# A feed-forward block in fp32: sums on VectorE, one buffer pool for both products, second factors form by form, and the finish written inside the last product

## The chip, the cores and the metric

The kernel runs on one core of a Trainium2 chip. The metric is the device time of one execution in microseconds (us). The core has TensorE (PE, matrix products into PSUM), VectorE (DVE), ScalarE (ACT), GpSimd (POOL), and SyncE (SP), whose queue issues the transfers between DRAM and SBUF here. The order of the instructions on each engine is fixed when the kernel is built, by the scheduler of the framework from the program's text, its priorities and its buffers; each engine takes its own instructions in that order and waits on semaphores for the others. PE runs at one of two clocks, 1.2 or 2.4 GHz; the profile shows the granted clock as a share of the higher one.

## The reference, cut to what matters

One encoder layer on x (1024 rows by 1024). The change touches the last of its three parts:

```python
h = _rms_norm(x, ffn_pre_norm)
gate, up = jnp.split(h @ w_ffn_in, 2, axis=-1)      # 1024 x 1024 by 1024 x 5632
y = (jax.nn.silu(gate) * up) @ w_ffn_out            # 1024 x 2816 by 2816 x 1024
x = x + _rms_norm(y, ffn_post_norm)
```

## The kernel before, in words

Each fp32 factor is split into two fp32r tiles, hi (a cast on ACT) and lo = raw - hi (a subtraction on DVE), and a product is hi*hi + lo*hi + hi*lo: three matmuls of 128x128 by 128x512. Both products use seven sub-products for eight (a Winograd form), so sums of blocks are needed in front of them and behind them.

First product, `ffn_in`: 22 groups (11 gate and up pairs), each a class `InGroup` with seven sub-products p1 to p7 of 12 matmuls. The weight's forms (A11, A12, A22, S1 to S4) are made for every group by `form` (hi L1382, lo L1383), their sums by POOL (L1402, 1403, 1409, 1413). The activation's forms (T1 to T4, B22) are made once by `FormSink.piece`, for each k of 4 in column pieces, with t1 and t3 on POOL and t2 and t4 on DVE. p1 and p2 of the first three groups need none of these and are done first (`first_forms`, `early = 3`). p1 is copied out by ACT (L1423) before p2 adds to the same PSUM bank. u1 (L1433), u2 (L1442) and the sums in `use` are DVE's. `send` writes seven activation forms of each pair to DRAM; its sums are POOL's (L1487 to L1497).

Second product, `ffn_out`: seven products n = 0 to 6 (A11*B11, A12*B21, S2*T2, S3*T3, S1*T1, A22*T4, S4*B22), each 11 steps over 4 row blocks j, 12 matmuls a step, 924 in all. `operands` loads an activation form (L1584), splits it (L1586 ACT, L1587 DVE), loads weight blocks, sums them on POOL for T1 to T4 (L1568 to L1579), and splits them (L1590 ACT, L1591 DVE). `use` adds a finished product from PSUM (L1619). In the last product `finish_tile` follows each j for rows 4+j and j: sum of squares (ACT), load of the residual (L1607), rstd (ten DVE instructions of 128x1, L73 to L80), a multiply by rstd and post norm on DVE (L1611), an add of the residual (L1612, POOL for one half of the columns, DVE for the other), and the store.

Ahead of `ffn_in` stands the last tile of `out_proj`: its norm and 16 transposes (L1068) give the last columns of the activation (hraw, evacuated by ACT, L1070). `ffn_in` and `ffn_out` have a pool of buffers each for activations and for weights.

Of the kernel before, what the change touches and what calls it, by code (L numbers as in the profile page):

```python
# [19 lines left out]
P = 128  # L20
# [1028 lines left out]
class FormSink:  # L1049
# [32 lines left out]
    def open(self, pl, n, k):  # L1082

        K = self.K
        for name in ("T1", "T2", "T3", "B22", "T4"):
            pair = []
            for p in "hl":
                if n:
                    pair.append(pl.tile([P, 512], F32R, name=f"x{name}{p}{k}"))
                    n -= 1  # L1090
                else:
                    pair.append(K.ap.tile([P, 512], F32R, tag="act", name="act_f", bufs=K.abufs))
            self.f.setdefault(name, []).append(tuple(pair))

    def piece(self, pl, k, s):

        K, nc = self.K, self.K.nc
        n = s.stop - s.start

        def put(name, k, src):  # L1100
            hi, lo = self.f[name][k]
            nc.scalar.copy(hi[:, s], src)
            nc.vector.tensor_sub(lo[:, s], src, hi[:, s].bitcast(F32))
        tmp = lambda name: pl.tile([P, n], F32, tag="as", name=name, bufs=3)
        b11, b12, b21, b22 = (self.raw[a][b][:, s] for a, b in ((k, 0), (k, 1), (k + 4, 0), (k + 4, 1)))
        t1, t2 = tmp("t1"), tmp("t2")
        nc.gpsimd.tensor_sub(t1, b12, b11)
        nc.vector.tensor_sub(t2, b22, t1)
        put("T2", k, t2)
        put("T1", k, t1)  # L1110
        t3 = tmp("t3")
        nc.gpsimd.tensor_sub(t3, b22, b12)
        put("T3", k, t3)
        t4 = tmp("t4")
        nc.vector.tensor_sub(t4, b21, t2)
        put("T4", k, t4)
        put("B22", k, b22)
# [229 lines left out]

def mmk(K, out, a, b, start):
# [10 lines left out]
class InGroup:  # L1359
# [6 lines left out]
    def __init__(self, K, fp, wp, hf, c0, use):  # L1366
        self.K, self.fp, self.wp, self.hf, self.c0, self.use = K, fp, wp, hf, c0, use
        self.w = {}

    def load(self):  # L1370
        K = self.K
        self.raw = []
        for kh in range(2):
            raw = self.wp.tile([P, 4, 256], F32, tag="wr", name="w_raw", bufs=3)
# [393 lines left out]
```

## Time and profile before

| | us |
|---|---|
| median of three runs (lowest, highest) | 2588.98 (2586.65, 2590.16) |
| the profiled execution, its own time | 2588.08 |
| its span | 2586.4 |
| first matmul of `ffn_in`, last one | 1874.72, 2325.03 |
| first matmul of `ffn_out`, last one | 2336.70, 2571.40 |

In the span 2467.4 us have PE busy. The part that the change touches is the last 712 us. All times below are microseconds from the span's start. A matmul's record lasts 0.39 us at full clock, but the next one starts 0.2269 us later; so PE's rate is read from starts. In the same way a row's duration on DVE or ACT overlaps the next row's by some 0.08 us, and the pitch from start to start is what a chain of them costs.

### The profile page before, as it was taken

Reading aid. Unit: us, or ns where it says so; the run is one execution under the profiler, and the core shown is the slowest. Engines: PE = TensorE matmul, PEld = TensorE weight load, DVE = VectorE, ACT = ScalarE, POOL = GpSimd, SP = SyncE. Lnnn points to the kernel's source line nnn. Section 1 sums busy time; section 2 is a strip of 40 time slices with the busy share of each in tenths; the row PEclk is TensorE's granted clock in tenths of the full one; section 3 lists DMA queues with packets and bytes.
Section 4 is the critical chain, followed back from the end, with each engine's and each line's share of the span. In section 5 each row is a group of like instructions: output and inputs, shape, how many; then the busy total and the mean of one; then the engine's idle time right before and its main releaser. Section 6 shows DMA issues by size and latency. Waiting matters only on the chain. (4 is left out here: it accounts for less than half of the span.)

```text
span 2586.4 us, 38885 instructions
## 1 busy us (share of the span) xinstructions
PE 2467.4 (95%) x13445; PEld 2011.7 (78%) x13445; DVE 1767.6 (68%) x4037; ACT 1068.3 (41%) x2807; POOL 747.0 (29%) x937
## 2 busy tenths in 40 slices
PE   7999999999999999999999999999979999998897
PEld 5787788788788777788877887887758888876776
DVE  7778787897887855765577567535596556645677
ACT  5236244544554534654463233223553333224343
POOL 3352111112111111422133014313154444422542
PEclk9999999999999999999999999999979999998999
DMA  6214323322322422412113323214333233318865
GB/s 200 86 46 122 77 52 76 101 57 67 97 61 62 97 69 86 135 54 73 62 61 112 105 87 129 97 49 139 111 118 114 94 106 106 102 61 285 278 217 173
DMA packets 294926, 273.12 MB, mean 106 GB/s; under 512 B 93344, under 2 KB 213961, under 8 KB 294729
## 3 DMA queue, kind: packets, MB, share of 16 engines
q1 hardware_dynamic: 294729, 270.64, 33.6%
q8 instruction: 106, 1.74, 0.3%
q14 instruction: 91, 0.75, 0.1%
HBM read 206.80 MB, written 63.77 MB: 105 GB/s over the span
## 5 line engine op out<-in xcount | busy, mean ns | idle before, releaser
L134 PE MATMUL mm<-act_hi,w_lo 128*128 128x512 f32 (+1 forms) x1216 | 481.1, 398 | 0.0
L133 PE MATMUL mm<-act_lo,w_hi 128*128 128x512 f32 (+1 forms) x1216 | 478.2, 395 | 0.0
L131 PE MATMUL mm<-act_hi,w_hi 128*128 128x512 f32 (+1 forms) x1216 | 332.1, 399 | 4.2 <-ACT act_hi L162 2.2
L115 POOL TENSOR_SCALAR w_hi<-w_raw 128x512 fp32r<-128x512 f32 x232 | 160.8, 708 | 410.8 <-PE mm L133 208.4
L134 PEld LDWEIGHTS mm<-act_hi,w_lo 128*128 128x128 f32 x1216 | 229.7, 189 | 37.4
L133 PEld LDWEIGHTS mm<-act_lo,w_hi 128*128 128x128 f32 x1216 | 229.5, 189 | 37.3
L131 PEld LDWEIGHTS mm<-act_hi,w_hi 128*128 128x128 f32 x1216 | 220.6, 190 | 45.2 <-ACT act_hi L162 3.1
L116 DVE TENSOR_TENSOR w_lo<-w_raw,w_hi 128x512 fp32r<-128x512 f32 x232 | 183.0, 808 | 59.7 <-POOL w_hi L115 52.8
L133 PE MATMUL mm<-w_lo,act_hi 128*128 128x512 f32 (+1 forms) x480 | 180.8, 382 | 0.0
L134 PE MATMUL mm<-w_hi,act_lo 128*128 128x512 f32 (+1 forms) x480 | 180.1, 381 | 0.0
L861 POOL TENSOR_SCALAR Pm<-Pm,sm 128x1024 f32<-128x1024 f32 (+1 forms) x96 | 89.1, 930 | 251.4 <-DVE sm L860 86.5
L459 DVE SCALAR_TENSOR_TENSOR acc<-xp,ccol,acc 128x1024 f32<-128x1024 f32 x96 | 124.0, 1292 | 4.6 <-ACT acc L456 3.7
L131 PE MATMUL mm<-w_hi,act_hi 128*128 128x512 f32 (+1 forms) x480 | 120.7, 387 | 3.7 <-POOL w_hi L115 2.6
L159 ACT CAST th<-tr 128x512 fp32r<-128x512 f32 x128 | 74.8, 588 | 105.5 <-PE tr L904 103.5
L1382 ACT CAST w_hi<-s 128x512 fp32r<-128x512 f32 x88 | 54.7, 622 | 146.4 <-PE g L1355 104.8
L133 PEld LDWEIGHTS mm<-w_lo,act_hi 128*128 128x128 f32 x480 | 91.6, 191 | 17.3
L134 PEld LDWEIGHTS mm<-w_hi,act_lo 128*128 128x128 f32 x480 | 91.5, 191 | 17.2
L131 PEld LDWEIGHTS mm<-w_hi,act_hi 128*128 128x128 f32 x480 | 86.1, 191 | 22.4 <-POOL w_hi L115 3.8
L160 DVE TENSOR_TENSOR tl<-tr,th 128x512 fp32r<-128x512 f32 x128 | 87.2, 684 | 17.5 <-ACT th L159 15.6
L1383 DVE TENSOR_TENSOR w_lo<-w_raw,w_hi 128x512 fp32r<-128x512 f32 x66 | 75.4, 1143 | 28.1 <-ACT w_hi L1382 28.0
L857 ACT ACTIVATE Pm<-sc,nm 128x512 f32<-128x512 f32 x128 | 87.1, 688 | 16.6 <-DVE nm L852 16.2
L850 DVE TENSOR_REDUCE mx<-sc 128x1 f32<-128x512 f32 x128 | 85.0, 681 | 4.3 <-PE sc L134 4.1
(474 smaller groups left out, 6120.2 us busy)
## 6 DMA issues: line engine op xcount, KB each, us to landing
w_raw<-in_w_ffn_out SPq DMA_DIRECT2D x121, 256.0 KB, 4.2
w_raw<-in_w_in SPq DMA_DIRECT2D x120, 256.0 KB, 3.2
w_raw<-in_w_ffn_in SPq DMA_DIRECT2D x50, 512.0 KB, 3.6
Gr<-grow SPq DMA_DIRECT2D x48, 256.0 KB, 3.5
a_raw<-afS SPq DMA_DIRECT2D x44, 256.0 KB, 3.4
afA<-sg SPq DMA_DIRECT2D x33, 256.0 KB, 2.0
afS<-as SPq DMA_DIRECT2D x33, 256.0 KB, 2.0
a_raw<-afA SPq DMA_DIRECT2D x33, 256.0 KB, 4.2
```

What stands on the lines that cost most here:

```text
L115: nc.gpsimd.tensor_scalar(hi[part], raw, 1.0, 1.0, op0=ALU.mult, op1=ALU.mult)
L116: nc.vector.tensor_sub(lo[part], raw, hi[part].bitcast(F32))
L131: nc.tensor.matmul(out, a[0], b[0], start=(i == 0), stop=False)
L133: nc.tensor.matmul(out, a[0], b[1], start=False, stop=False)
L134: nc.tensor.matmul(out, a[1], b[0], start=False, stop=(i == n - 1))
L159: nc.scalar.copy(hi, ps)
L160: nc.vector.tensor_sub(lo, ps, hi.bitcast(F32))
L459: nc.vector.scalar_tensor_tensor(acc, xp[:, j:j + T], tap(j), acc, op0=ALU.mult, op1=ALU.add)
L850: nc.vector.reduce_max(mx[:, j:j + 1], ps, axis=AX.X)
L857: nc.scalar.activation(Pm[:, j * w:(j + 1) * w], ps, AF.Exp, bias=nm, scale=scale, accum_out=sm[:, j:j + 1])
L861: nc.gpsimd.tensor_scalar(Pm, Pm, sm[:, 0:1], 1.0, op0=ALU.mult, op1=ALU.mult)
L1383: nc.vector.tensor_sub(lo, src, hi.bitcast(F32))
```

## The change

Five edits. All sums of the block go to VectorE, so POOL has nothing to do in it. One pool, "ffn", gives the buffers for both products (a ring of 48 tiles of 128x512, and three weight tiles for `ffn_in`). `FormSink` makes the second factors form by form: T2 of all four k, then T1, T3, T4 and B22, once for the first 256 columns and once for the last 256; before, it went k by k, and k = 2, 3 at full width. In `ffn_out` T1 is kept from the step that makes T2, so that product 4 loads 22 weight blocks fewer (99 for 121), and the post norm is loaded behind product 3. The finish is split: `square` (sum of squares, load of the residual, a multiply by post norm) and `finish_tile` (rstd and one instruction that multiplies by it and adds the residual); rows 4 to 7 and the first halves of rows 0 to 3 are written into the last product's loop.

```diff
+    def first_piece(self, s):
+        nc = self.K.nc
+        self.t = [ffn_tile(self.K, "t12") for k in range(4)]
+        for k in range(4):
+            b11, b12, b21, b22 = self.blocks(k, s)
+            t1, t2 = self.t[k][:, 0:256], self.t[k][:, 256:512]
+            nc.vector.tensor_sub(t1, b12, b11)
+            nc.vector.tensor_sub(t2, b22, t1)
+            self.put("T2", k, s, t2)
...
-        nc.gpsimd.tensor_add(s1, self.block(1, 0), self.block(1, 1))
-        nc.gpsimd.tensor_sub(s2, s1, self.block(0, 0))
+        nc.vector.tensor_add(s1, self.block(1, 0), self.block(1, 1))
+        nc.vector.tensor_sub(s2, s1, self.block(0, 0))
...
     groups[0].p1()
     groups[0].p2()
-    for k in range(2):
-        hf.open(fp, 10 - 8 * k, k)
-        hf.piece(fp, k, first)
+    hf.open()
+    hf.first_piece(first)
+    hf.other_pieces(first)
     finish()
     for G in groups[1:early]:
         G.p1()
         G.p2()
-    for k in range(2):
-        hf.piece(fp, k, last)
-    for k in range(2, 4):
-        hf.open(fp, 0, k)
-        hf.piece(fp, k, both)
+    hf.first_piece(last)
+    groups[0].forms()
+    hf.other_pieces(last)
...
+        if name == "T2":
+            t1[g], t2[g] = half_tile(K, "t1"), ffn_tile(K, "t2")
+            nc.vector.tensor_sub(t1[g], weight(g, 0, 1), weight(g, 0, 0))
+            nc.vector.tensor_sub(t2[g], weight(g, 1, 1), t1[g])
+            return t2[g]
...
+    def square(t, ch):
+        part = acc[t // 4, ch, t % 4]
...
+        row_ssq(K, part, ssq[t][:, ch:ch + 1], xt[t, ch])
+        nc.sync.dma_start(xt[t, ch], K.x2[t * P:(t + 1) * P, ch * 512:(ch + 1) * 512])
+        nc.vector.tensor_mul(part, part, post[ch])
+
     def finish_tile(t):
...
+        rs = rstd1(K, ssq[t])
         for ch in range(2):
...
+            o = xt[t, ch]
+            nc.vector.scalar_tensor_tensor(o, acc[t // 4, ch, t % 4], rs, o, op0=ALU.mult, op1=ALU.add)
...
             for j in range(4):
                 ps = banks[n % 2][j](K)
                 for g, (a, b) in enumerate(ab):
                     step(ps, j, a, b, g)
+                if j == 0:
+                    second_half(4)
+                    for t in range(4):
+                        square(t, 0)
                 use(n, j, ps)
-                finish_tile(4 + j)
+                square(j, 1)
                 finish_tile(j)
+                if j < 3:
+                    second_half(5 + j)
...
-        with pool(K, "ffi") as fp, pool(K, "ffiw", "right") as wp:
-            ffn_in(K, sink, finish, fp, wp)
-        with pool(K, "ffo") as fp, pool(K, "ffow", "right") as wp:
-            ffn_out(K, fp, wp, out)
+        with pool(K, "ffn") as K.fp:
+            ffn_in(K, sink, finish)
+            ffn_out(K, out)
```

In the rows that follow, lines of the kernel after have their own numbers: L1404 is the cast of a weight form, L1095 and L1096 the cast and the lo of an activation form, L1441 the copy of p1, L1485 the silu of the first gate block, L1609 to L1611 the matmuls of `ffn_out`, L1621 the multiply by post norm, L1627 the multiply and add of the finish, L1634 the add of a finished product.

ScalarE where `ffn_in` begins, before (hraw are the evacuated last columns, p the copies of p1, t and hraw what activation forms are cast from):

```order
L1070 ACTIVATE hraw<-tr,cols 128x256 x5
L1382 CAST w_hi<-w_raw 128x512
L1423 COPY p_19939<-mm 128x512
L1102 CAST xT2h_19957<-t_19966 128x256
L1102 CAST xT1h_19955<-t_19965 128x256
L1382 CAST w_hi<-w_raw 128x512
...
L1467 ACTIVATE sg<-mm 128x512
L1102 CAST act_f<-t_19994 128x256
L1423 COPY p_20052<-mm 128x512
L1102 CAST act_f<-t_20001 128x256
L1423 COPY p_20080<-mm 128x512
```

The same place after:

```order
L1070 ACTIVATE hraw<-tr,cols 128x256 x8
L1404 CAST w_hi<-w_raw 128x512 x6
L1441 COPY p_19936<-mm 128x512
L1485 ACT_TABLE_LOAD
L1485 ACTIVATE sg<-mm 128x512
L1095 CAST part<-t_19992 128x256
L1095 CAST act_f<-t_19993 128x256
...
L1095 CAST part<-t_19995 128x256
L1095 CAST part<-hraw 128x256 x6
L1441 COPY p_20093<-mm 128x512
L1441 COPY p_20121<-mm 128x512
```

The casts of activation forms moved from in front of the first silu to behind it, and the copies of p1 for the second and third group moved behind all 24 casts of the first 256 columns.

TensorE in the last product, before (mm_25350 is the bank of j = 0, mm_25435 of j = 1; the two steps at the end of j = 0 and the start of j = 1):

```order
L1596 MATMUL mm_25350<-w_hi_25346,act_hi_25340 128x512
L1597 MATMUL mm_25350<-w_lo_25347,act_hi_25340 128x512
L1598 MATMUL mm_25350<-w_hi_25346,act_lo_25341 128x512
L1596 MATMUL mm_25435<-w_hi_25226,act_hi_25220 128x512
L1597 MATMUL mm_25435<-w_lo_25227,act_hi_25220 128x512
L1598 MATMUL mm_25435<-w_hi_25226,act_lo_25221 128x512
```

The same product after (mm_25274, mm_25399, g_25479 and tr_25559 are the banks of j = 0 to 3):

```order
L1609 MATMUL mm_25274<-w_hi_25150,act_hi_25146 128x512
L1609 MATMUL mm_25399<-w_hi_25150,act_hi_25146 128x512
L1609 MATMUL g_25479<-w_hi_25150,act_hi_25146 128x512
L1609 MATMUL tr_25559<-w_hi_25150,act_hi_25146 128x512
L1610 MATMUL mm_25274<-w_lo_25151,act_hi_25146 128x512
L1611 MATMUL mm_25274<-w_hi_25150,act_lo_25147 128x512
```

Before, a row block took its 33 matmuls one after the other; now every step goes over all four, and the four sums end within the last eight matmuls.

VectorE at the end of the last product, after (u and c are parts of rows 4 to 7 and of the first halves, one the sums that the last product completes, h and r the small tiles of rstd):

```order
L1621 TENSOR_TENSOR c_23902<-c_23902,post 128x512
L77 TENSOR_SCALAR h_25317<-h_25317 128x1
L1621 TENSOR_TENSOR c_23904<-c_23904,post 128x512
L79 SCALAR_TENSOR_TENSOR h_25317<-r_25318,h_25317 128x1
L1634 TENSOR_TENSOR one<-mm,one 128x512
L80 SCALAR_TENSOR_TENSOR r_25318<-h_25317,r_25318 128x1
L73 TENSOR_SCALAR h_25358<-ssq_25333 128x1
L1634 TENSOR_TENSOR one<-mm,one 128x512
```

The first add of the last product stands behind six multiplies and five small instructions of the finish; the other 10 multiplies, 75 small instructions and all 16 multiply-and-adds stand behind it.

## Rows read from the trace of the kernel before

**Rows 1.** The page: busy time and share of each engine, and the span in 40 slices for PE and its granted clock.

```profile
PE 2467.4 (95%) x13445; PEld 2011.7 (78%) x13445; DVE 1767.6 (68%) x4037; ACT 1068.3 (41%) x2807; POOL 747.0 (29%) x937
PE   7999999999999999999999999999979999998897
PEclk9999999999999999999999999999979999998999
```

**Rows 2.** Windows of the last part: the stretch and its length, then busy us and instructions of each engine, the granted clock, the DMA engines' share and GB/s.

```profile
1895.00:1900.00 5.00, 5.00 (x23) 3.94 (x21) 4.37 (x9) 2.57 (x9) 2.73 (x4) 1.00 0.33 105
1900.00:1935.00 35.00, 21.14 (x61) 13.59 (x61) 35.00 (x42) 15.85 (x30) 22.28 (x15) 0.71 0.24 76
1950.00:2000.00 50.00, 50.00 (x222) 41.44 (x221) 31.80 (x38) 15.56 (x26) 25.99 (x19) 1.00 0.34 116
2340.00:2345.00 5.00, 5.00 (x17) 3.92 (x17) 3.77 (x7) 3.58 (x6) 0.00 (x0) 0.68 0.98 364
2410.00:2415.00 5.00, 2.97 (x7) 2.08 (x8) 5.00 (x6) 3.22 (x6) 4.97 (x4) 0.50 0.30 109
```

**Rows 3.** What PE waited for from 1870 to the end: the waiter, what released it, us in total, times, longest.

```profile
PE mm L1596 <- ACT w_hi L1590: 11.3, 1, 11.3
PE mm L1596 <- ACT act_hi L1586: 11.0, 4, 7.4
PE g L1353 <- ACT w_hi L1382: 5.6, 2, 5.2
PE mm L1598 <- DVE act_lo L1587: 3.1, 2, 2.2
```

**Rows 4.** The timeline of DVE from 1895: start, duration, line, operation, output and inputs.

```profile
1897.55 0.42 DVE L1103 TENSOR_TENSOR act_f<-t,act_f 128x256 fp32r<-128x256 f32 x1
1897.89 0.42 DVE L1103 TENSOR_TENSOR xT1l<-t,xT1h 128x256 fp32r<-128x256 f32 x1
...
1904.99 0.68 DVE L1383 TENSOR_TENSOR w_lo<-s,w_hi 128x512 fp32r<-128x512 f32 x1
1905.60 0.68 DVE L1108 TENSOR_TENSOR t<-hraw,t 128x512 f32<-128x512 f32 x1
...
1908.82 1.75 DVE L1383 TENSOR_TENSOR w_lo<-s,w_hi 128x512 fp32r<-128x512 f32 x1
```

**Rows 5.** The timeline of POOL at the same time as the last of these rows.

```profile
1908.31 1.71 POOL L1413 TENSOR_TENSOR s<-w_raw,s 128x512 f32<-128x512 f32 x1
```

**Rows 6.** The timelines of PE and of ACT where `ffn_in` begins; in brackets the idle time before, and what ended it.

```profile
1885.24 1.38 PE L1068 MATMUL tr<-ident,y 128*128 128x128 f32 x8
...
1900.53 0.50 PE L1353 MATMUL g<-xT2h,w_hi 128*128 128x512 f32 x1 [0.36 <-ACT w_hi L1382]
...
1933.02 0.50 PE L1353 MATMUL g<-xT4h,w_hi 128*128 128x512 f32 x1 [1.13 <-DVE u L1442]
```

```profile
1887.90 0.62 ACT L1382 CAST w_hi<-w_raw 128x512 fp32r<-128x512 f32 x1
...
1891.71 1.28 ACT L1467 ACT_TABLE_LOAD   x1
1893.01 0.60 ACT L1467 ACTIVATE sg<-mm 128x512 f32<-128x512 f32 x1
```

**Rows 7.** The timeline of PE where products of `ffn_out` begin (their first matmul and what it waited for), and the last matmul of `ffn_in`.

```profile
2325.03 0.39 PE L1356 MATMUL tr<-act_f,w_lo 128*128 128x512 f32 x1
...
2336.70 0.80 PE L1596 MATMUL mm<-w_hi,act_hi 128*128 128x512 f32 x1 [11.29 <-ACT w_hi L1590]
...
2371.62 0.50 PE L1596 MATMUL mm<-w_hi,act_hi 128*128 128x512 f32 x1 [1.53 <-ACT act_hi L1586]
...
2412.03 0.79 PE L1596 MATMUL mm<-w_hi,act_hi 128*128 128x512 f32 x1 [7.43 <-ACT act_hi L1586]
2412.62 0.63 PE L1597 MATMUL mm<-w_lo,act_hi 128*128 128x512 f32 x1
2413.05 0.63 PE L1596 MATMUL mm<-w_hi,act_hi 128*128 128x512 f32 x1
```

**Rows 8.** The timelines of PE and of DVE at the end of the last product: the last matmul and the fifteenth before it, small instructions of two rstd chains in turn (the first and the last of 13 rows, and the row that follows) and of one chain alone (neighbours), the multiplies of the finish, and the last add.

```profile
2568.00 0.39 PE L1598 MATMUL tr<-w_hi,act_lo 128*128 128x512 f32 x1
...
2571.40 0.39 PE L1598 MATMUL tr<-w_hi,act_lo 128*128 128x512 f32 x1
```

```profile
2550.86 0.16 DVE L75 SCALAR_TENSOR_TENSOR h<-ssq,h 128x1 f32<-128x1 f32 x1 [0.79 <-ACT xf L218]
...
2552.66 0.15 DVE L77 TENSOR_SCALAR h<-h 128x1 f32<-128x1 f32 x1
2552.78 0.75 DVE L1611 SCALAR_TENSOR_TENSOR c<-c,r,post 128x512 f32<-128x512 f32 x1
2553.45 0.75 DVE L1611 SCALAR_TENSOR_TENSOR one<-one,r,post 128x512 f32<-128x512 f32 x1
...
2576.63 0.68 DVE L1619 TENSOR_TENSOR one<-tr,one 128x512 f32<-128x512 f32 x1
...
2579.57 0.16 DVE L80 SCALAR_TENSOR_TENSOR r<-h,r 128x1 f32<-128x1 f32 x1
2579.76 0.22 DVE L79 SCALAR_TENSOR_TENSOR h<-r,h 128x1 f32<-128x1 f32 x1
2580.01 0.16 DVE L80 SCALAR_TENSOR_TENSOR r<-h,r 128x1 f32<-128x1 f32 x1
...
2581.72 1.58 DVE L1612 TENSOR_TENSOR xf<-xf,one 128x512 f32<-128x512 f32 x1
```

**Rows 9.** DMA issues of the page: output and input, count, KB each, median us from issue to landing.

```profile
w_raw<-in_w_ffn_out SPq DMA_DIRECT2D x121, 256.0 KB, 4.2
w_raw<-in_w_ffn_in SPq DMA_DIRECT2D x50, 512.0 KB, 3.6
```

More of the change, by code (lines that the diff above doesn't have):

```diff
@@ L1080, in split, with open @@
         return hi, lo
-    def open(self, pl, n, k):
+    def open(self):
         K = self.K
[L1085 to L1117, printed above, removed]
+        n = 0
@@ new lines, in open, with put, blocks @@
+        for k in range(4):
+            for name in ("T2", "T1", "T3", "T4", "B22"):
+                of = act_part if 10 <= n < 26 else ffn_part
+                self.f.setdefault(name, []).append((of(K), of(K)))
+                n += 2
+    def put(self, name, k, s, src):
+        hi, lo = self.f[name][k]
+        self.K.nc.scalar.copy(hi[:, s], src)
+        self.K.nc.vector.tensor_sub(lo[:, s], src, hi[:, s].bitcast(F32))
+    def blocks(self, k, s):
+        return (self.raw[a][b][:, s] for a, b in ((k, 0), (k, 1), (k + 4, 0), (k + 4, 1)))
@@ new lines, in first_piece, with other_pieces @@
+    def first_piece(self, s):
+        nc = self.K.nc
+        self.t = [ffn_tile(self.K, "t12") for k in range(4)]
+        for k in range(4):
+            b11, b12, b21, b22 = self.blocks(k, s)
[3 more added lines that the diff above has]
+            self.put("T2", k, s, t2)
+    def other_pieces(self, s):
+        nc = self.K.nc
+        for k in range(4):
+            self.put("T1", k, s, self.t[k][:, 0:256])
+        for k in range(4):
+            b11, b12, b21, b22 = self.blocks(k, s)
+            nc.vector.tensor_sub(self.t[k][:, 0:256], b22, b12)
+            self.put("T3", k, s, self.t[k][:, 0:256])
+        for k in range(4):
+            b11, b12, b21, b22 = self.blocks(k, s)
+            nc.vector.tensor_sub(self.t[k][:, 256:512], b21, self.t[k][:, 256:512])
+            self.put("T4", k, s, self.t[k][:, 256:512])
+        for k in range(4):
+            self.put("B22", k, s, self.raw[k + 4][1][:, s])
@@ L1421, in p1 @@
         mmk(self.K, self.a, self.w["A11"], self.hf["B11"], True)
-        self.one = self.small("p1", 3)
+        self.one = self.tile_("p1")
         self.K.nc.scalar.copy(self.one, self.a)
@@ L1508, in ffn_in @@
     groups[0].p2()
-    first, last, both = slice(0, 256), slice(256, 512), slice(0, 512)
-    for k in range(2):
-        hf.open(fp, 10 - 8 * k, k)
-        hf.piece(fp, k, first)
+    first, last = slice(0, 256), slice(256, 512)
+    hf.open()
+    hf.first_piece(first)
+    hf.other_pieces(first)
     finish()
@@ L1537, in ffn_in, with ffn_out @@
     prev.p3()
-def ffn_out(K, fp, wp, out):
+def ffn_out(K, out):
     nc = K.nc
@@ L1587, in operands @@
         nc.vector.tensor_sub(al, ar, ah.bitcast(F32))
-        w = second(sec, g)
-        wh, wl = (wp.tile([P, 512], F32R, tag="wf", name=f"w_{p}", bufs=24) for p in ("hi", "lo"))
+        wh, wl = (ffn_tile(K, f"w_{p}", F32R) for p in ("hi", "lo"))
         nc.scalar.copy(wh, w)
@@ L1651, in ffn_out, with second_half @@
                 use(n, j, ps[j])
+            if n == 3:
+                for ch in range(2):
+                    post.append(half_tile(K, "post"))
+                    nc.sync.dma_start(post[ch], K.i["ffn_post_norm"][:, ch * 512:(ch + 1) * 512].to_broadcast([P, 512]))
         else:
             ab = [operands(first, sec, g) for g in range(NG)]
+            def second_half(t):
+                square(t, 0)
+                square(t, 1)
+                finish_tile(t)
             for j in range(4):
```

115 lines of the change are left out of this document (53 added, 62 removed).

## The prediction

> **What bounds the kernel now.** I read the page first. PE is busy for 95% of the span, and nearly every slice shows it at 9 tenths at full clock [rows 1]. So only the stretches where PE stands still can be gained, and whatever stands between the last matmul and the end. The windows of the last part come next. In the middle of the first product PE is busy for 50.00 of 50 us and DVE for 31.80, so DVE and POOL have slack there [rows 2]. At its start it is otherwise: from 1900 to 1935 DVE is busy for all 35.00 us, PE for 21.14 at a mean clock of 0.71 [rows 2]. Then the list of PE's waits: one of 11.3 where the second product begins, four of 11.0 together where later products begin, 3.1 for lo tiles there, and 5.6 for a weight form at the start [rows 3]. Last the timeline of the end: the last matmul starts at 2571.40, the last add ends at 2583.30, the span at 2586.4 [rows 8]: 15.0 us in which DVE is the chain.
>
> So four stretches decide: start of the first product, its middle, the second product, the end. PE's pitch is 3.40 us for 15 matmuls, 0.227 each [rows 8].
>
> **The cost of DVE's instructions.** A 128x256 subtraction has a pitch of 0.34 us, a 128x512 one 0.61 [rows 4]. While POOL has a sum in hand the 128x512 one takes 1.75 [rows 4, 5]. The change takes POOL's sums away, so I count DVE at 0.34 and 0.61 throughout. The Trainium skill says that VectorE and GpSimd share a pair of SBUF ports as an exclusive lock, held for a whole instruction (SBUF — State Buffer, Who interferes with whom). The trace agrees with it (1.75 beside POOL's 1.71). By that rule alone the change could only gain; that is the first rival below.
>
> **Start of the first product.** Before, PE does p1 and p2 of three groups by about 1900, starts p6 at 1900.53 and p4 of the first group at 1933.02, with 120 matmuls behind it (six early products, then p6, p5, p7 and the second group's p6, 12 each), and then runs at full rate [rows 6]. After, ACT's order is different (the fences on ScalarE): six casts, a copy, one silu, 24 half casts, and only then the copies of p1 that p2 of groups two and three wait for. I follow that chain.
> - The six weight tiles of 512 KB take the place of out_proj's buffers or wait for the split of the first three. The transposes begin at 1885.24 [rows 6]; a load takes 3.6 [rows 9], cast and lo 0.6 each: 1885 + 3.6 + 1.2 + 3.6 = 1893.4 for the last one.
> - Its cast 0.6, the copy 0.6, p2 of group one with what is left of p1 (18 matmuls, 4.1), silu 0.6 and the first half cast 0.4: DVE can begin its chain of lo tiles at about 1899.7. The table load (1.28, [rows 6]) lies beside p2.
> - 38 half subtractions at 0.34 are 12.8: 1912.5, with the copy 1913. PE stood idle for some 14 us, so p2 of group two runs at least in part at the low clock (a 0.43 pitch after a wait, [rows 7]): 4.5, to 1917.5.
> - DVE's next instruction is the product of that p2 with the silu, and the second half of the columns stands behind it. From there the S2 sum needs 5.5 (1923), its cast and lo 1, p6 and p5 5.4 (1929.5). DVE still has 19 halves (6.4) and 9 whole ones (5.5) from 1923, so u1 comes at 1935, p7 2.7 and u2 0.7: p4 of group one at 1939.3, with 108 behind it.
> That is 6.3 later and 12 matmuls (2.7) fewer, +9.0; in two of the next groups p4 stands right behind p7 and waits 0.8 for u2: +10.6. From below: by DVE's work alone (first rival) -3.6. From above: all of p2's 24 matmuls cold and a load each late by its 3.6 gives +16.
>
> **Middle.** Each gate and up pair needs about 40 DVE instructions after, 24.4 us at 0.61, against 168 matmuls or 38.1 us. PE stays the bound; an in-order wait may cost 0 to 2. I take +0.5.
>
> **Second product.** From the last matmul of the first product (2325.03, [rows 7]) to the last one of all are 246.4 us; 924 matmuls are 209.7. So 36.7 is lost: 25.4 in waits [rows 3], the rest to the low clock behind them (0.68 and 0.50, [rows 2]; pitch 0.43 behind the wait of 7.43, [rows 7]). After, one pool lets SP load the first operands while the first product still runs, and ACT cast them; what is left of each wait is what DVE and ACT have in front of the first lo or cast:
> - the last group's adds and the sums for DRAM, 8 whole instructions: 4.7;
> - four copies and a cast on ACT: 1.7;
> - four adds, t1, t2 and a cast less what PE still has queued: 2.9;
> - four adds, one sum, a cast: 2.3; then 0.6, 1.7 and 1.2 for the products with two, eight and four adds, most of them covered by steps already split.
> These are 15.1, with some 4 for the clock 19.1, against 36.7: -17.6. In the product that makes T2 DVE has four instructions a step, 2.4 against PE's 2.7, and the loads are 1 MB a step: at 364 GB/s [rows 2] 2.9 us, 1.8 too slow over eleven steps, which the six steps ahead cover. If no operand comes ahead, the first 11.3 stays and the term is -11; with no clock loss it is -22.
>
> **The end.** This is the part that speaks against the change. The diff writes rows 4 to 7 into the last product, but the order puts them elsewhere: PE goes over all four row blocks in each step (the fences on TensorE), so the four sums end with the last matmuls. On DVE the first add of such a sum has only six multiplies and five small instructions of the finish in front of it (the fence on VectorE). Behind it stand 4 adds and 10 multiplies at 0.61 (8.5), 16 multiply-and-adds at 0.67 (10.7; the pitch of L1611, [rows 8]) and 75 small ones. Those took 1.92 for 13 with two chains in turn, 0.148 each, and 0.22 in one chain alone [rows 8]: 75 by 0.148 are 11.1. Together 30.3. They begin 0.9 before the last matmul's start, and from the last DVE instruction to the end are 3.1 as before: 32.5 against 15.0, +17.5; I take +17, since small instructions also hide behind large ones (0.10 each gives +14, 0.22 gives +22). ACT's ten squares and the loads of the residual run ahead of DVE. The Trainium skill calls ACT's and DVE's queues strict first in, first out (TensorE: Matmul & The Clock Gate, the architectural detail on the array, engine queue depths). The trace bears that out: the add of the last sum, whose matmul started at 2571.40, runs at 2576.63 behind the finish of earlier rows [rows 8]. Could DVE pass the waiting add, the 13 us or so of rows 4 to 7 would lie beside matmuls and the end would cost +4.
>
> **The sum.** 10.6 + 0.5 - 17.6 + 17 = +10.5 on the profiled execution's own 2588.08: 2598.6. The median of the runs is 0.9 above that execution, so I forecast 2599.
>
> **The rivals.**
> 1. *DVE set free.* From 1900 to 1935 DVE was stretched by POOL all the time [rows 2, 5]. Its 42 instructions there (32 whole, 10 halves) would take 22.9 alone, POOL's 15 added 9: 31.4 and not 35. If amount decides and not order, the start gains 3.6, the second product loses only its 15.1 of waits (-22), the end costs +14 or +17: -8 to -11, about 2580. For it: every DVE row beside POOL is two and a half times as long. Against: the chain above has DVE waiting for PE twice. It decides if p4 of group one starts before 1933. The sharing rule of the Trainium skill (SBUF — State Buffer, Who interferes with whom) points the same way.
> 2. *The gains and losses cancel.* The start costs 5 (loads earlier, no cold p2), the end 14, the second product gains 19: within 5 us of before, 2584 to 2594.
> 3. *Nothing comes ahead.* The ring of 48 tiles is full of the first product's forms until it ends; the transition stays at 11.3 and T2's loads, 2.9 a step, bind: the second product gains 9 at most, the start costs 14: about 2610. For it: 4.2 us a load [rows 9]. Against: the forms of the last groups leave the ring before the end.
> 4. *The finish does lie inside the product*, as the diff says: the end costs -2 and the sum is 2580. The order on PE excludes nearly all of it.
>
> **How the numbers follow.** About 5 us, 0.2%, is what a measurement of this kernel can tell from no change. Chances: forecast 0.50 (2594 to 2606), rival 1 0.20, rival 2 0.14, rival 3 0.13, rival 4 0.03. Faster 0.23 (rivals 1 and 4); same 0.14 (rival 2); slower 0.63. The forecast's own range is 2594 to 2606. To hold the time 8 times in 10 the range has to reach rival 1 on one side and rival 3 on the other: 2579 to 2612. Left out are rival 4 and the far ends of the other cases, some 0.15.
>
> **What would show it.** In the profile after: PE idle for more than 10 us between p2 of group one and p2 of group two near 1900 to 1913; p4 of the first group near 1939; POOL with no sums and DVE's 128x512 rows at 0.68 throughout; the first matmul of the second product within 6 us of the last of the first; and more than 30 us between the last matmul and the end, with DVE busy through all of it. I am wrong in the start if PE never idles over 5 us there, in the second product if more than 25 or less than 13 us are lost, and in the end if it is under 27 us.

## The result and the profile after

The changed kernel takes 2613.78 us, median of 4 runs (2612.78 to 2614.59), beside 2589.46 for the kernel before in the same job: a ratio of 1.0096, 95% interval 1.0078 to 1.0113. The forecast was 2599 with a range of 2579 to 2612: the sign was right, and the time lies outside the range. The profiled execution has a span of 2612.34 us.

To compare profiles I cut the span at three points: the transposes of h that follow a wait of 2.2 us for POOL (1872.85 in the profile before, 1877.01 after), the last matmul of the first product, and the last matmul of all. What lies ahead of the first point is the same code in all kernels here, and in the profiled executions of the kernels below that point stands anywhere from 1874.1 to 1882.8. The kernel before alone ran between 2586.7 and 2597.1 us over all jobs. So I take the 4.2 us by which the point differs here as scatter between executions; with one profile of each kernel that is not shown.

| stage, us | before | after | difference | forecast |
|---|---|---|---|---|
| transposes to last matmul of the first product | 452.2 | 468.1 | +15.9 | +11.1 |
| to the last matmul of all | 246.4 | 238.8 | -7.6 | -17.6 |
| to the end | 15.0 | 28.4 | +13.4 | +17 |
| sum | 713.5 | 735.3 | +21.8 | +10.5 |

The page after (busy us, and the granted clock in 40 slices), which answers to [rows 1]. POOL has lost 291 us of work and DVE gained only 21:

```profile
PE 2472.2 (95%) x13445; PEld 2015.9 (77%) x13445; DVE 1788.5 (68%) x4251; ACT 1063.3 (41%) x2817; POOL 455.7 (17%) x730
...
PEclk9999999999999999999999999999889999999998
```

Windows after (busy us and instructions of each engine, granted clock, DMA share, GB/s), against [rows 2]: the stretch in which PE stands, the middle, and the end, in which DVE is busy for 26.12 of 29.90 us:

```profile
1900.00:1916.00 16.00, 3.79 (x17) 2.82 (x15) 12.88 (x39) 9.87 (x28) 0.00 (x0) 0.75 0.18 61
1916.00:1947.00 31.00, 21.51 (x61) 16.07 (x62) 18.82 (x46) 9.46 (x23) 0.00 (x0) 0.74 0.13 43
1950.00:2000.00 50.00, 48.00 (x209) 38.61 (x207) 33.47 (x54) 13.60 (x25) 0.00 (x0) 1.00 0.32 104
...
2582.40:2612.30 29.90, 1.94 (x9) 1.29 (x7) 26.12 (x105) 6.35 (x20) 0.00 (x0) 0.58 0.65 228
```

What PE waited for from 1870 to the end, against [rows 3]. The wait of 11.3 at the second product's beginning has become one of 0.7 and, two matmuls on, one of 3.8; a wait of 12.2 for a copy and one of 8.4 in front of the transposes are new:

```profile
PE mm L1374 <- ACT p L1441: 12.2, 1, 12.2
PE tr L1068 <- POOL y L1030: 10.6, 2, 8.4
PE mm L1611 <- DVE act_lo L1601: 8.4, 3, 3.8
PE mm L1609 <- ACT w_hi L1603: 6.7, 4, 3.3
PE g L1374 <- ACT w_hi L1404: 5.6, 1, 5.6
```

PE's timeline at the start, against [rows 6]: the transposes, p1 of group one (1874.72 before), p2 of group two, p6, and p4 of group one:

```profile
1885.81 1.54 PE L1068 MATMUL tr<-ident,y 128*128 128x128 f32 x6 [8.36 <-POOL y L1030]
...
1891.04 2.07 PE L1374 MATMUL mm<-act_hi,w_hi 128*128 128x512 f32 x4 [1.43 <-ACT w_hi L1404]
...
1916.02 2.07 PE L1374 MATMUL mm<-act_hi,w_hi 128*128 128x512 f32 x4 [12.23 <-ACT p L1441]
...
1929.99 0.80 PE L1374 MATMUL g<-part,w_hi 128*128 128x512 f32 x1 [5.58 <-ACT w_hi L1404]
...
1946.74 0.47 PE L1374 MATMUL g<-part,w_hi 128*128 128x512 f32 x1 [0.87 <-DVE u L1460]
```

DVE at the same time. Its chain of lo tiles for the first half of the forms begins at 1903.39; it waits 5.32 for p2 of group two, and then 2.07 for a half cast. That cast stood on ACT behind the third group's silu (1924.45, in front of which ACT waited 8.00 for PE):

```profile
1903.39 0.43 DVE L1096 TENSOR_TENSOR part<-t,part 128x256 fp32r<-128x256 f32 x1 [3.12 <-ACT part L1095]
...
1921.54 0.69 DVE L1495 TENSOR_TENSOR sg<-sg,mm 128x512 f32<-128x512 f32 x1 [5.32 <-PE mm L1377]
...
1925.98 0.42 DVE L1096 TENSOR_TENSOR part<-t,part 128x256 fp32r<-128x256 f32 x1 [2.07 <-ACT part L1095]
```

```profile
1924.45 0.60 ACT L1485 ACTIVATE sg<-mm 128x512 f32<-128x512 f32 x1 [8.00 <-PE mm L1377]
```

PE where products of the second part begin, against [rows 7]: the first product's last matmul, the first of the second product 1.1 us later, and the six longest waits that are left:

```profile
2345.14 0.39 PE L1377 MATMUL tr<-part,w_lo 128*128 128x512 f32 x1
2346.23 0.50 PE L1609 MATMUL mm<-w_hi,act_hi 128*128 128x512 f32 x1 [0.70 <-ACT act_hi L1600]
...
2350.77 0.79 PE L1611 MATMUL mm<-w_hi,act_lo 128*128 128x512 f32 x1 [3.81 <-DVE act_lo L1601]
...
2417.31 1.22 PE L1609 MATMUL mm<-w_hi,act_hi 128*128 128x512 f32 x2 [3.29 <-ACT w_hi L1603]
...
2455.76 0.50 PE L1609 MATMUL mm<-w_hi,act_hi 128*128 128x512 f32 x1 [3.06 <-ACT w_hi L1603]
...
2488.41 0.50 PE L1611 MATMUL mm<-w_hi,act_lo 128*128 128x512 f32 x1 [1.51 <-DVE act_lo L1601]
...
2521.24 0.50 PE L1611 MATMUL mm<-w_hi,act_lo 128*128 128x512 f32 x1 [3.08 <-DVE act_lo L1601]
...
2555.03 0.50 PE L1610 MATMUL mm<-w_lo,act_hi 128*128 128x512 f32 x1 [1.51 <-DVE w_lo L1604]
```

DVE in front of and inside the product that makes T2. It stands 17.30 us before an add that waits for the product before, and then does a step in 3.24 us (2423.76 to 2427.01 to 2430.25), of which 0.74 is a wait for ACT's cast of t2. PE's 12 matmuls take 2.72:

```profile
2412.01 0.69 DVE L1634 TENSOR_TENSOR c<-mm,one 128x512 f32<-128x512 f32 x1 [17.30 <-PE mm L1611]
...
2423.76 0.69 DVE L1604 TENSOR_TENSOR w_lo<-t,w_hi 128x512 fp32r<-128x512 f32 x1 [0.74 <-ACT w_hi L1603]
2424.37 0.69 DVE L1585 TENSOR_TENSOR t<-w_raw 128x512 f32<-128x512 f32 x1
2424.98 0.69 DVE L1601 TENSOR_TENSOR act_lo<-a_raw,act_hi 128x512 fp32r<-128x512 f32 x1
2425.58 0.69 DVE L1586 TENSOR_TENSOR t<-w_raw,t 128x512 f32<-128x512 f32 x1
2427.01 0.69 DVE L1604 TENSOR_TENSOR w_lo<-t,w_hi 128x512 fp32r<-128x512 f32 x1 [0.74 <-ACT w_hi L1603]
...
2430.25 0.69 DVE L1604 TENSOR_TENSOR w_lo<-t,w_hi 128x512 fp32r<-128x512 f32 x1 [0.74 <-ACT w_hi L1603]
```

The end, against [rows 8]: DVE waits 12.01 for the first of the last sums, and PE's last matmul is 0.9 us behind it:

```profile
2583.02 0.69 DVE L1634 TENSOR_TENSOR one<-mm,one 128x512 f32<-128x512 f32 x1 [12.01 <-PE mm L1611]
```

```profile
2583.95 0.39 PE L1611 MATMUL tr<-w_hi,act_lo 128*128 128x512 f32 x1
```

### The profile page after: what moved, and what is told of

It is laid out like the page before. It is cut to its first block, busy times and chain, and to the rows that moved or that the text cites. A ratio compares the mean times of both kernels' runs of the same rounds, so it can differ in the third digit from the quotient of the medians.

```text
span 2612.3 us, 38718 instructions
## 1 busy us (share of the span) xinstructions
PE 2472.2 (95%) x13445; PEld 2015.9 (77%) x13445; DVE 1788.5 (68%) x4251; ACT 1063.3 (41%) x2817; POOL 455.7 (17%) x730
## 4 chain that ended last, share of the span: by engine, by line
PE 51%; DVE 5%; ACT 2%; issue 1%; DMA 1%; POOL 1%; DVEq 0%; POOLq 0%; SPq 0%; ACTq 0%
PE mm L133 6%; PE mm L134 6%; PE mm L131 6%; PE g L1374 2%; PE g L1376 2%; PE g L1377 2%; PE tr L904 2%; PE mm L1374 2%; PE mm L1377 2%; PE mm L1376 2%; PE tr L1374 1%; PE tr L1376 1%; PE tr L1377 1%; PE mm L1611 1%; PE av L922 1%
## 5 line engine op out<-in xcount | busy, mean ns | idle before, releaser
L116 DVE TENSOR_TENSOR w_lo<-w_raw,w_hi 128x512 fp32r<-128x512 f32 x232 | 184.0, 813 | 60.6 <-POOL w_hi L115 53.8
L1404 ACT CAST w_hi<-s 128x512 fp32r<-128x512 f32 x88 | 54.1, 623 | 158.2 <-PE g L1376 101.6
L643 DVE TENSOR_TENSOR Ly<-Ly,tmp 128x240 f32<-128x240 f32 (+27 forms) x248 | 82.7, 334 | 3.2
```

The lines of the kernel that those rows point to most:

```text
L116: nc.vector.tensor_sub(lo[part], raw, hi[part].bitcast(F32))
```

## The experiments

Theory A: VectorE and ScalarE work in a written order, and at four places an instruction that waits for TensorE, or for the other of the two, stands in front of ready work. Rival B: the amount of VectorE's work, or loads and space, is the bound. Each run was timed beside the kernel before on the same chip, whose median was 2590.7 (e1 to e4), 2592.0 (e5 to e8), 2593.0 (e9 to e11) and 2591.1 (e12). Since that median moves by up to 3.5 us from job to job, small differences between runs of different jobs are read from the ratios. The stages of each profile:

| run | first product | second | end | median us | ratio to before, 95% |
|---|---|---|---|---|---|
| before | 452.2 | 246.4 | 15.0 | 2589.5 | |
| after | 468.1 | 238.8 | 28.4 | 2613.8 | 1.0078 to 1.0113 |
| e1_t2 | 468.4 | 238.8 | 28.4 | 2614.2 | 1.0072 to 1.0103 |
| e2_ahead | 468.3 | 221.2 | 28.4 | 2596.7 | 1.0007 to 1.0026 |
| e3_finish | 467.9 | 238.7 | 24.2 | 2611.0 | 1.0063 to 1.0088 |
| e4_start | 466.8 | 238.3 | 28.4 | 2614.8 | 1.0075 to 1.0101 |
| e5_finish2 | 467.5 | 241.1 | 20.0 | 2604.6 | 1.0038 to 1.0062 |
| e6_own_pool | 464.3 | 241.5 | 28.4 | 2611.1 | 1.0064 to 1.0088 |
| e7_sums_gpsimd | 481.4 | 232.3 | 28.4 | 2618.6 | 1.0080 to 1.0114 |
| e8_row_by_row | 468.2 | 247.6 | 11.4 | 2604.0 | 1.0037 to 1.0061 |
| e9_forms_first | 465.9 | 243.1 | 28.4 | 2612.1 | 1.0062 to 1.0089 |
| e10_together | 465.5 | 213.6 | 16.3 | 2572.1 | 0.9910 to 0.9937 |
| e11_all | 464.8 | 213.7 | 16.3 | 2571.2 | 0.9902 to 0.9931 |
| e12_halves | 452.7 | 213.6 | 16.3 | 2561.9 | 0.9865 to 0.9903 |

**The second product.** e1 changes VectorE's order in a step of T2:

```diff
+        if sec == "T2":
+            with K.tc.issue_after(K.t2_ins):
+                nc.vector.tensor_sub(al, ar, ah.bitcast(F32))
```

> The only edit: in the product that makes T2, VectorE's order in a step is t1, t2, act_lo, w_lo instead of t1, act_lo, t2, w_lo. TensorE's and ScalarE's orders stay. Theory A (hand-overs in a fixed order set the pace: VectorE stands 0.74 us in each step for ScalarE's cast of t2): act_lo fills that gap, the step falls from 3.24 to about 2.72 us, TensorE's own pace for 12 matmuls, and the run gains 4 to 6 us on 2613.8: about 2609. Rival B (VectorE's amount of work or the loads of 1 MB a step set the pace): the step stays at 2.9 us or more, the gain is under 3 us. The tail of 29.9 us and the start stay as they are by both.

DVE's step fell as A has it, to 2.76 us (three w_lo of e1):

```profile
2425.66 0.69 DVE L1608 TENSOR_TENSOR w_lo<-t,w_hi 128x512 fp32r<-128x512 f32 x1
...
2428.42 0.69 DVE L1608 TENSOR_TENSOR w_lo<-t,w_hi 128x512 fp32r<-128x512 f32 x1
...
2431.18 0.69 DVE L1608 TENSOR_TENSOR w_lo<-t,w_hi 128x512 fp32r<-128x512 f32 x1
```

T2's product took 34.90 instead of 38.45 us, but the total did not move. The 3.55 us came back as 2.7 in the next product (32.81 against 30.07) and 1.2 in a later one (36.09 against 34.89). PE was busy through the next product in both kernels, behind a wait of 3.1 in both, but its granted clock was 0.90 in e1, a mean between its two levels of 1.2 and 2.4 GHz, and 1.00 after (PE busy, clock, DMA share, GB/s; first e1, then after):

```profile
2457.80:2488.00 30.20, 30.18 (x121) 0.90 0.67 217
```

```profile
2455.70:2485.80 30.10, 30.04 (x132) 1.00 0.73 241
```

So the shorter step is shown, its gain in the total is not. With e9, whose second part has the same code as the changed kernel, taking 243.1 us against 238.8, a difference under 4 us in this stage proves nothing by itself. Held against e9, where the same two products were as slow as in e1 (32.78 and 36.06 us at 0.91, in both kernels), e1's second product is 4.3 us shorter, 3.5 of it in the product that makes T2 (34.90 against 38.40). So between these two profiles the gain is there, and beside the changed kernel's profile the lower clock hides it.

e2 leaves the amount of work and takes the adds out of the way:

```diff
-                a, b = operands(first, sec, g)
+                a, b = ops.pop((n, g), None) or operands(first, sec, g)
...
+            for g in range(3):
+                ops[n + 1, g] = operands(*products[n + 1], g)
             for j in range(4):
                 use(n, j, ps[j])
```

> The only edit: the operands of the first three steps of the next product (two casts and two lo tiles each, and its sum) are written ahead of the four adds that finish the product before. The amount of work stays. Theory A (the wait at each product's beginning is VectorE standing in front of adds that wait for TensorE's last matmuls, with ready operand work queued behind them): the waits of 3.3, 3.1, 1.5, 3.1 and 1.5 us where products three to seven begin fall under 1 us each and some low clock goes with them: 9 to 13 us less, about 2603. Rival B (the operands come late because loads or slots of the buffers are late, or because VectorE has too much to do): the waits go to other places, and the gain is under 4 us.

The second product fell by 17.7 us and the time by 17.1, more than A expected. One of the five waits that A named did not fall, the 3.07 in front of the fourth product: there the scheduler's order still has adds of the product before (from 2441.25) in front of the first sum for T3 (2444.25). PE's waits there, those over 0.6 us each, went from 18.2 (eight) to 8.5 us (four); T2's product, with steps ready ahead, took 30.1 beside its wait instead of 35.4; the remaining 2.7 I put down to low clock that no longer follows (products four to six take 29.9 to 30.1, which is 132 matmuls at 0.227). On DVE the step of T2 in e2 keeps its 3.24 and its 0.74, but the first steps are done before the add that waits, and not behind it:

```profile
2395.52 0.69 DVE L1604 TENSOR_TENSOR w_lo<-t,w_hi 128x512 fp32r<-128x512 f32 x1 [0.69 <-ACT w_hi L1603]
...
2398.76 0.69 DVE L1604 TENSOR_TENSOR w_lo<-t,w_hi 128x512 fp32r<-128x512 f32 x1 [0.74 <-ACT w_hi L1603]
...
2410.65 0.69 DVE L1634 TENSOR_TENSOR c<-mm,one 128x512 f32<-128x512 f32 x1 [9.39 <-PE mm L1611]
```

B falls for this stage. The Trainium skill calls ACT's and DVE's queues strict first in, first out (TensorE: Matmul & The Clock Gate, the architectural detail on the array, engine queue depths); the 17.30 in front of L1634 after, and the 17.7 us that the same work gains in front of it, agree.

**The end.** The expectations put it at 29.9 us, counted from 2582.40; from the start of the last matmul, as in the table, it is 28.4. e3 puts the finish of rows 4 to 7 ahead of every add of the last sums, e5 ahead of the first of them only (`if j == 0`), e8 sends TensorE row block by row block:

```diff
-                    second_half(4)
+                    for t in range(4, 8):
+                        second_half(t)
...
-                use(n, j, ps)
+                with K.tc.issue_after(K.fin):
+                    use(n, j, ps)
```

```diff
-                    step(ps, j, a, b, g)
+                    if g == 0 and j:
+                        with K.tc.issue_after(K.last):
+                            step(ps, j, a, b, g)
+                    else:
+                        step(ps, j, a, b, g)
```

> The only edit: on VectorE the first add of a sum of the last product stands behind the finish of rows 4 to 7 instead of in front of it. TensorE's order stays. Theory A (the tail is long because that add waits for TensorE's last matmuls while the finish of rows 4 to 7 is ready behind it): the finish of rows 4 to 7 lies beside the last product's matmuls and the time from the last matmul to the end falls from 29.9 to between 15 and 19 us: 11 to 15 us less, about 2600. Rival B (the finish of rows 4 to 7 is itself late, because its sums, its residual loads or ScalarE's squares come late): the tail falls by under 6 us. Rival C: the finish in the product delays the operands there and TensorE loses several us inside the product, though the tail is short.

> As in the run before, the finish of rows 4 to 7 stands on VectorE ahead of the first add of the last product's sums, but the four adds and the finishes of rows 0 to 3 are left free to alternate, where that run put one row behind the other. Theory A (that run's tail of 24.2 us was four chains of 5.3 us in series, each with a wait for ScalarE's square and small instructions that follow one another): with the chains side by side the tail is 4 adds, 4 multiplies and 8 multiply-and-adds (10.2 us), some 28 small instructions at 0.10 (2.8) and 3 to 4 us to the end: 15 to 18 us against 29.9, so 11 to 14 us less: about 2601. Rival B (the finish of rows 4 to 7, which ended just before the last matmul there, holds the adds back): the tail stays above 21 us.

> Undoes one part: in the last product TensorE goes row block by row block (all eleven steps of one, then the next), as before the change; what VectorE is given stays. Theory A (the tail is long because the four sums end together): the first sum is ready some 20 us before the last matmul, the tail falls from 29.9 to between 15 and 19 us; the first row block needs all eleven steps' operands at VectorE's 1.2 us a step against TensorE's 0.7, so TensorE waits 4 to 7 us more inside the product: 5 to 10 us less in all, near 2606. Rival B (VectorE's work in the last product is too much for it in either order): the tail stays above 24 us.

e3 missed: the end fell by 4.2 us only. Its finish of rows 4 to 7 did lie inside the product, but my edit put the last four rows in series, 5.3 to 5.4 us each, as the adds of e3 show:

```profile
2583.95 0.68 DVE L1634 TENSOR_TENSOR one<-mm,one 128x512 f32<-128x512 f32 x1
2589.34 0.68 DVE L1634 TENSOR_TENSOR one<-mm,one 128x512 f32<-128x512 f32 x1
2594.66 0.68 DVE L1634 TENSOR_TENSOR one<-g,one 128x512 f32<-128x512 f32 x1
2600.03 0.68 DVE L1634 TENSOR_TENSOR one<-tr,one 128x512 f32<-128x512 f32 x1
```

With that freed, e5 ends 20.0 us behind the last matmul and is faster than the changed kernel by 9 us in the medians and 12 in the ratios (1.0050 against 1.0096). The end lies between A (15 to 18) and B (over 21); the finish of one of rows 4 to 7 still ran at 2585.72, ahead of the last add. e8 has the shortest end, 11.4 us, at the price that A named: its last product takes 38.3 us instead of 31.7. Each of the two is worth 9 to 12 us, and the order on the engines is what made the end long.

**The start.** e4 writes p1 and p2 of groups two and three ahead of the forms of h. e6 gives the raw weight tiles and the first group's hi and lo forms a pool of their own, e9 gives one to the raw tiles alone (the forms go into the ring of the act tiles) and writes the forms of the first columns ahead of groups two and three:

```diff
-        with pool(K, "ffn") as K.fp:
+        with pool(K, "ffnw", "right") as K.fw, pool(K, "ffn") as K.fp:
...
-            raw = K.fp.tile([P, 4, 256], F32, tag="wr", name="w_raw", bufs=3)
+            raw = K.fw.tile([P, 4, 256], F32, tag="wr", name="w_raw", bufs=3)
```

```diff
-    for G in groups[:early]:
-        G.first_forms()
+    groups[0].first_forms()
     groups[0].p1()
-    groups[0].p2()
     first, last = slice(0, 256), slice(256, 512)
     hf.open()
     hf.first_piece(first)
     hf.other_pieces(first)
+    groups[0].p2()
+    for G in groups[1:early]:
+        G.first_forms()
```

> The only edit: p1 and p2 of groups two and three are written ahead of the forms of h, so that ScalarE does their copies before its 24 half casts. TensorE's order stays. By the step of the prediction (TensorE idles 12 us because the copies of p1 stand behind 24 half casts) the start gains 8 to 11 us: about 2604. Rival (the 24 casts and VectorE's 38 half subtractions have to be done before p6 in any case, so the idle time is only moved: TensorE no longer waits 12 us in front of p2 of group two but in front of p6): within 2.5 us of 2613.8 either way, and the start of p4 of group one stays within 2.5 us of 1946.7.

> Undoes one part for the first group alone: its raw weight tiles and the four tiles of its hi and lo forms lie in a pool of their own on the side that is free while out_proj still runs, as before; the common ring has 44 tiles instead of 48. Theory A (the start is late because the first loads and forms wait for out_proj's buffers): p1 of group one begins near 1878 instead of 1891 (1875 before the change), in the 8.4 us in which TensorE waits for the last transposes; ScalarE's casts and silu come 4 to 6 us earlier, and so does p4 of group one: about 4 to 6 us less, near 2609. Rival B (the 24 casts and 38 half subtractions of the forms, which need the last part of h, set the start): p1 comes early, p4 of group one moves by less than 2 us, and the time by less than 2 us.

> On top of the run with the first group's own tiles (here its raw tiles in a pool of their own, its hi and lo forms in the ring of the act tiles, so that the common ring keeps 48): the forms of h for the first columns are written ahead of the first forms and of p1, p2 of groups two and three. So ScalarE's 24 half casts and VectorE's 38 half subtractions begin right behind the last of h (near 1887) and not behind six casts, a copy and a silu (1902.5). Theory A (the beginning of this block of forms sets when p6 and p4 of group one can run, since the block is some 13 us of VectorE in any order): p4 of group one near 1930 instead of 1946.7, 10 to 15 us less, about 2601. Rival B (groups two and three then come late by as much, or the second half of the columns is the bound): p4 of group one not before 1938, under 6 us less.

e4: the rival held. PE no longer waits 12.2 in front of p2 but 19.1 in front of p6; counted from the transposes, p6 comes 51.3 us later (53.0 after, 27.7 before), and p4 68.4 (69.7 after). e6: p1 of group one ran at 1876.65, between the transposes, and p4 of group one came 3.8 us earlier (66.0 from the transposes, 69.7 after): the late space is worth some 4 of the start's 16 us. The second product is 2.7 us longer in e6, but not at its beginning: there PE waited 3.61 once, where after it waited 0.70 and 3.81. The difference lies in the fourth and sixth products (31.70 against 30.07, 36.06 against 34.89), at a granted clock of 0.95 and 0.91 against 1.00 and 0.95; so a cost of the ring of 44 is not shown. e9 missed by A's numbers, and its rival held: counted from the transposes, VectorE did the first half of the forms 11.7 us earlier, and still p4 came at 67.5, no better than e6. ACT of e9 shows why. The casts of groups two and three now stood behind the forms, one of them waited for its load, and the third group's silu for p2, with the second half of the forms behind it:

```profile
1910.13 0.62 ACT L1407 CAST w_hi<-w_raw 128x512 fp32r<-128x512 f32 x1 [4.24 <-DMA w_raw<-in_w_ffn_in]
1916.22 0.58 ACT L1444 COPY p<-mm 128x512 f32<-128x512 f32 x1 [4.99 <-PE mm L1377]
1919.93 0.60 ACT L1488 ACTIVATE sg<-mm 128x512 f32<-128x512 f32 x1 [3.13 <-PE mm L1377]
```

**The sums.** e7 gives GpSimd its sums back, in both products, their forms and the sums for DRAM:

```diff
-        nc.vector.tensor_add(s1, self.block(1, 0), self.block(1, 1))
+        nc.gpsimd.tensor_add(s1, self.block(1, 0), self.block(1, 1))
...
-                nc.vector.tensor_sub(t1[g], weight(g, 0, 1), weight(g, 0, 0))
+                nc.gpsimd.tensor_sub(t1[g], weight(g, 0, 1), weight(g, 0, 0))
```

> Undoes one part: every sum of weights and of h that the change took from GpSimd is on GpSimd again (first product, its forms, the sums for DRAM, second product); pools and order of the forms stay as changed. Theory A (what VectorE's added work costs is little, what GpSimd beside it costs is more): VectorE's 128x512 subtractions take 1.7 us beside a sum on GpSimd again, the start loses 3 to 6 us more, and the product that makes T2 takes over 3.3 us a step: 5 to 15 us slower than 2613.8. Rival B (the move of the sums to VectorE is itself what costs the 24 us): back near 2595.

Neither theory held for the whole: in the profiles the first product got 13.3 us longer and the second 6.5 shorter. The time is not told apart from the changed kernel's (ratios 1.0097 and 1.0096), so the loss of 5 to 15 us that A expected is not shown. At the start DVE's 128x512 subtractions lie at 0.68 alone and up to 1.76 beside POOL. The sharing rule that the prediction took from the Trainium skill (SBUF — State Buffer, Who interferes with whom) agrees with the trace on the duration, and on the first product; in the second, sums beside it on GpSimd went with a shorter time all the same. I put that down to DVE's queue, the narrow place there, having less to do; no run separates it. That run's rival B falls: undoing the move does not bring the time back. No run undoes the 22 weight blocks that are no longer loaded, or the common pool for the second product alone; what these two are worth is not shown.

**Together.** e10 joins e2 and e6 (the forms in the ring of the act tiles, the common ring of 48 kept), sends the first two row blocks of the last product step by step together and the others in turn, and writes the first three operands of the second product ahead of the last group's adds. e11 adds e9's order. e12 adds to that the order of the second cut below; the first cut is of e10, with its last two lines against e8:

```diff
+    for g in range(3):
+        ops[0, g] = operands(*products[0], g)
+    yield
...
-                    if g == 0 and j:
+                    if g == 0 and j > 1:
```

```diff
     finish()
-    for G in groups[1:early]:
-        G.p1()
-        G.p2()
+    groups[1].first_forms()
     hf.first_piece(last)
+    groups[1].p1()
+    groups[1].p2()
     groups[0].forms()
+    groups[2].first_forms()
     hf.other_pieces(last)
+    groups[2].p1()
+    groups[2].p2()
```

> All parts that the runs so far bear out, and one new: operands of three steps ahead of the adds between products, and also ahead of the last group's adds in the first product; the first group's raw tiles and forms in space of their own (forms in the ring of the act tiles); in the last product the first two row blocks step by step together, then the third, then the fourth. If each part keeps its own gain: -17 (operands ahead), -3 (the 3.8 us where the second product's first lo tile is late), -4 (start), and in the last product -12 to -17 (tail near 11.4 us, and under 3 us of waits, since two row blocks take 1.36 us a step against VectorE's 1.2): 2572 to 2580, below the kernel before (2589 to 2592). If the gains overlap (VectorE's finish of rows 4 to 7 now runs against the operands): 2585 or more.

> The kernel of all parts together with the forms of the first columns ahead of groups two and three as well. If the start is set by when that block begins, it gains the same 10 us more that it gains alone: 2562 to 2570. If that run alone gains nothing, this one is level with the one without it.

> On top of all parts together: the second half of the columns of T2 and the first group's further weight forms no longer stand behind p1, p2 of groups two and three; the third group's first forms, p1 and p2 are written behind them, so that TensorE has p6 and p5 of group one between p2 of groups two and three. Theory A (in the start VectorE and ScalarE stand in front of what waits for p2 of groups two and three: 3.6 and 5.2 us idle on VectorE at 1911 to 1921 in the run with the forms first): p6 of group one comes 8 to 13 us earlier than 1922 (upstream shift taken off), p4 follows near 1928 to 1932, and the time is 7 to 10 us under the two runs before: 2561 to 2565. Rival B (the raw weights' three tiles and their loads set the start): p6 not before 1918, within 3 us of 2571.5.

e10 came to 2572.1, where the gains add up, although its end is 16.3 us and not 11.4; its second product takes 213.6 us against 209.7 for its 924 matmuls at 0.227. e11 is level with it, as e9 alone had been level with e6. e12 confirmed A for the start: p6 comes 37.8 us behind the transposes (49.8 in e9), p4 54.3 (before 60.2), and the time is 2561.9, a ratio to the kernel before of 0.9884 (0.9865 to 0.9903). PE of e12 has its one long wait in front of group two, then p2 of group three at 1925.47, p7 and p4:

```profile
1907.65 2.07 PE L1374 MATMUL mm<-act_hi,w_hi 128*128 128x512 f32 x4 [12.54 <-ACT w_hi L1407]
...
1925.47 1.20 PE L1374 MATMUL mm<-act_hi,w_hi 128*128 128x512 f32 x4 [0.91 <-ACT p L1444]
...
1932.64 0.47 PE L1374 MATMUL g<-part,w_hi 128*128 128x512 f32 x1 [0.88 <-DVE u L1463]
```

## Why the prediction was right in sign and wrong in size

- **The second product: the step that failed** (-17.6 forecast, -7.6 measured, 10 of the 11.3 us that the sum was short). The forecast left a loss of 19.1 us there: 15.1 of waits and 4 of clock. Measured are 29.1: 18.2 of waits, 5.4 of T2's pace, and 5.5 that I put down to the clock. The waits are 3 of the 10 us: the first four came nearly as forecast (0.7 and 3.8 for 4.7, 1.2 for 1.7, 3.3 for 2.9, 3.1 for 2.3). The clock is 1.5. The largest part is the 5.4 of T2's pace, which the sum put at nothing: e1 takes 3.6 of it away by another order in the step, e2 all of it by steps ahead. Two sentences failed. "DVE has four instructions a step, 2.4 against PE's 2.7" counted work and left out the hand-over: t2 goes to ACT for its cast and back, 0.74 us in each step with DVE idle. And "the six steps ahead cover" took for granted that steps would stand ahead: the adds stood in front of them, and e2 shows what they hold back. The last three waits, most of which "steps already split" were to cover, are 1.5, 3.1 and 1.5 us in full, 6.1 where the sum had 3.5.
- **The start: mechanism right, 4.8 us too small** with the middle (+11.1 forecast, +15.9 measured). PE idles 12.23 us where the forecast had more than 10, for the copy behind the half casts. Counted from the transposes p4 of group one is 9.6 later, not 6.3: the second half of the forms stood behind the third group's silu, which the chain had left out, and p6 to p7 ran at a granted clock of 0.74. The trace has 15 matmuls fewer ahead of p4, 3.4 us (12 and 2.7 forecast, from a count of 120 before, which is 123). The waits for u2 behind it cost 1.7 more than before (1.6 forecast), and 1.3 is left for the middle (0.5 forecast).
- That the copies behind the casts are the cause was the wrong half of this step: e4 took them away, and the idle time moved on. The start is a ring of hand-overs among PE, ACT and DVE, and only e12, which cuts it at both halves of the forms, gets it back.
- **The end: right in place, 3.6 us too large** (+17 forecast, +13.4 measured). DVE's 105 instructions, 30 large and 75 small, are there as counted. They fill 26.1 us: the small ones cost 0.10 beside large ones, the lower of the two prices the forecast gave (+14), and not 0.148.
- **The rivals.** *DVE set free* had the durations right (0.68 everywhere) and the outcome wrong: p4 did not start before 1933. Its "every DVE row beside POOL" was misread: before, of the 22 whole rows on DVE that overlap one of POOL's between 1895 and 1935, 11 took 1.2 to 1.8 us and the others 0.7 to 0.9. *Nothing comes ahead* gave the nearest time, 2610, but by a mechanism that did not occur: the first wait of the second product fell from 11.3 to 0.7 and 3.8. That it came near is luck. *Finish inside the product* did not occur, and e5 and e8 show that it was within reach. *Gains and losses cancel* fell with the second product (7.6 gained, not 19) and the start (15.9, not 5).
- Of what would prove me wrong, the second product did: 29.1 us lost, where I had put the limit at 25. The end, 28.4 us, stayed above the 27 that would have refuted it, under the 30 that I expected.

## What to carry to other kernels

Before counting an engine's instructions, find in its order the first one that waits for another engine, and list what is ready behind it: here that list, not the amount of work, was worth 17 us in one place, 9 in a second and some 10 in a third. Work that is passed to another engine and back in every step costs the hand-over as well as the instructions, unless something independent stands between. And one idle time that is removed by moving what it waits for may only move; in a ring of hand-overs all the links have to be looked at together.

## What was not expected

- The same wait in front of the same matmul was followed by a granted clock of 1.00 in one kernel and 0.90 over the next 30 us in another (3.1 us in both, after and e1). This moved the second product by up to 4 us between kernels with the same code there.
- A hand-over from DVE to ACT and back left DVE idle for 0.74 us in each step, more than the 0.61 that a 128x512 subtraction takes of its time.
- With sums on GpSimd beside it, DVE's subtractions were up to 2.6 times as long (e7, 1.76 us against 0.68 at the start), and the second product was still 6.5 us shorter.
- The part of the kernel ahead of the change, the same code throughout, ended at times up to 10 us apart in the profiled executions (1872.85 to 1882.84).
